# The low part of K on all 128 partitions, and a smaller copy of V that shares a buffer

## The chip, the cores and the metric

The kernel runs on one core of a Trainium2 chip. The metric is device time in microseconds (us), the median of several executions; lower is better.

## The reference, cut to what matters

A trunk of two layers on 1024 tokens of width 1024, float32. Layer 0 is a short gated convolution beside a state-space scan, layer 1 is attention with a forget gate; each is followed by a layer norm, a convolutional feed-forward network and another layer norm. The change touches layer 1 alone:

```
h = x @ w_in                                  # q, k, v of 16 heads of 64, and a forget logit per head
cum = cumsum(log_sigmoid(f_logit + b_f))      # per head, along the tokens
s = (q . k) / 8 + cum[query] - cum[key]       # keys after the query masked
o = softmax(s) @ v                            # per head
mixer = o @ w_out
```

## The kernel before, in words

**Operands.** TensorE multiplies float32r operands. Each float32 operand of a large product is held as the sum of a high and a low part; a projection makes three products (high by high, high by low, low by high).

**Attention.** `attention` takes the 16 heads in 8 pairs. `projections` (L610) computes q, k and v of a pair as [128 channels, 1024 tokens], two heads of 64 channels one above the other, in halves of 512 tokens, each half in one PSUM bank (`place`). `evacuations` (L572) turns such a half into operands:
- q: for each head a tile of 128 partitions, the high part on the head's own 64, the low part on the other 64.
- k: for each head a tile `kh` whose 64 rows of the high part stand on both halves of the partitions (L599, L600), and one tile `kl` for the pair, with each head's low part on the head's own 64 partitions.
- v: a copy `vc` on ScalarE (L586), four transposes on TensorE (L589), and the split into a high and a low part.

`scores(pr, e, i)` (L646) makes the scores of 128 queries (tile i, 0 to 7) of head e of pair pr against the first (i + 1) * 128 keys, in parts of up to 512 columns. A first pass multiplies q's tile of 128 rows by `kh`, which gives q times the high part of K. A second pass multiplies 64 rows, q's high part, by `kl`. A last product of 128 columns adds the causal mask (L660). All go to the one buffer `wide`, which VectorE reads at L663 (bias added, minimum taken); ScalarE takes the exponential, GpSimd divides by the sum.

`weigh` transposes these probabilities in groups of up to four through two small PSUM buffers (`sm`) and splits them into `p`, high on ScalarE and low on VectorE. `values` (L688) multiplies them by v, through the same small buffers; ScalarE copies half of the result to a scratch `ot` (L701), and VectorE adds the other half to it (L702).

**Order.** A loop over the 128 tiles issues the scores of tile n, the transposes of tile n - 2 (`LAG`), and P @ V of tile n - 4 (`VLAG`); steps of four products from the projections, and in the last pair from part of the output projection, are put between them (36 steps a pair, running `LEAD` = 12 steps ahead). The order of the instructions on each engine is then settled by the tile scheduler when the program is built, which may move independent instructions past each other; in the trace, P @ V stands between the scores and the mask of some tiles. Each engine runs its own instructions in order.

**Buffers.** A tag of a pool has a fixed number of slots. Before: `kl` two of 4 KB a partition, `vc` one of 4 KB, `ot` two of 1 KB; `kh` and `q` three of 4 KB each. `places_of` (L745) gives the slots that the last projections and heads leave free to the operands of the output projection's last pairs.

Of the kernel before, what the change touches and what calls it, by code (L numbers as in the profile page):

```python
# [10 lines left out]
F32 = mybir.dt.float32  # L11
F32R = mybir.dt.float32r
# [17 lines left out]
LAG, VLAG = 2, 4    # tiles of 128 tokens by which the transposes and P @ V follow the scores  # L30
XLAG = 2            # tiles by which the transposes into x.T follow the layer norm
LEAD = 12           # steps by which the projections run ahead of the heads
FILL, FILL7 = 36, 72  # steps of products between the heads of a pair, and of the last pair


class Net:
    """The trunk. Every float32 operand of a large product is held as the exact sum of
    two float32r parts, high and low; a product takes the passes hh, hl and lh."""
# [56 lines left out]
    def split(self, high, low, src, engine=None):  # L95
        """high + low == src exactly."""
        self.nc.scalar.copy(high, src)  # L97
        (engine or self.nc.vector).tensor_sub(low, src, high.bitcast(F32))  # L98
# [19 lines left out]
    def project(self, *srcs):  # L118
        """[128 channels, L] = W[:, 128 channels].T @ x.T for each slice of W; several go
        side by side over the rows of x.T."""  # L120
        nc = self.nc
        ws = [src if isinstance(src, (tuple, list)) else self.weight(src) for src in srcs]
        ps = [self.mm_ps() for _ in srcs]
        steps = [(half, k, t, n) for k in range(KD) for t in range(len(srcs)) for n in range(3) for half in range(2)]
        if self.fresh > 0:
            self.fresh -= len(srcs)
            steps.sort(key=lambda s: s[0])
        for half, k, t, n in steps:
            if half:
                while self.after:  # L130
                    self.after.pop(0)()
            h, l = ws[t]
            w, x = ((h, self.xh), (h, self.xl), (l, self.xh))[n]
            hs = slice(half * 512, half * 512 + 512)
            nc.tensor.matmul(ps[t][:, hs], lhsT=w[:, k * P:(k + 1) * P], rhs=x[:, k, hs],  # L135
                             start=(k == 0 and n == 0), stop=(k == KD - 1 and n == 2))
        return ps if len(srcs) > 1 else ps[0]

    def conv(self, out, ps, w, bias=None):
        """Causal depthwise convolution along the free axis; w[:, K] by channel."""  # L140
        nc = self.nc
        K = w.shape[-1]
        if bias is None:
            nc.scalar.activation(out, ps, AF.Copy, scale=w[:, K - 1:K])
        else:
            nc.scalar.activation(out, ps, AF.Identity, scale=w[:, K - 1:K], bias=bias)  # L146
        for s in range(1, K):
            nc.vector.scalar_tensor_tensor(out=out[:, s:], in0=ps[:, :L - s], scalar=w[:, K - 1 - s:K - s],  # L148
                                           in1=out[:, s:], op0=ALU.mult, op1=ALU.add)

    def down(self, ys, ws, evac, late=0):
        """evac(i, psum) for each tile i of 128 tokens of y @ W; what it returns is called after the
        products of the next tile or, after the last tiles, beside the next projection. The last ones
        of ys may come late."""
        nc = self.nc
        n = len(ys)
        blocks = [range(3)] + [[i] for i in range(3, NT)] if late else [[i] for i in range(NT)]
        after = self.after
        for block in blocks:
            ps = {i: self.mm_ps() for i in block}  # L160
            for js in (range(n - late), range(n - late, n)):
                for i in block:
                    for j in js:
                        (yh, yl), (wh, wl) = ys[j], ws[j]
                        for m, (y, w) in enumerate(((yh, wh), (yh, wl), (yl, wh))):
                            for hs in (slice(0, 512), slice(512, D)):
                                nc.tensor.matmul(ps[i][:, hs], lhsT=y[:, i * P:(i + 1) * P], rhs=w[:, hs],  # L167
                                                 start=(j == 0 and m == 0), stop=(j == n - 1 and m == 2))
            while len(after) > XLAG - 1:
                after.pop(0)()  # L170
            after += [then for then in [evac(i, ps[i]) for i in block] if then]

    def log1p_exp_neg_abs(self, x, tmp):
        """log1p(exp(-|x|)) / 2, by 2 atanh(e / (2 + e))."""
        nc, V = self.nc, self.nc.vector
        e, d, z, p = tmp
        nc.scalar.activation(e, x, AF.Abs)
        nc.scalar.activation(e, e, AF.Exp, scale=-1.0)
        V.tensor_scalar_add(d, e, 2.0)
        V.reciprocal(d, d)  # L180
        V.tensor_mul(d, d, e)
        V.tensor_mul(z, d, d)
        V.tensor_scalar_mul(p, z, 1.0 / 17)
        for c in (15, 13, 11, 9, 7, 5, 3):
            V.scalar_tensor_tensor(out=p, in0=p, scalar=1.0 / c, in1=z, op0=ALU.add, op1=ALU.mult)
        V.scalar_tensor_tensor(out=p, in0=p, scalar=1.0, in1=d, op0=ALU.add, op1=ALU.mult)
        return p
# [6 lines left out]
    def thin_weight(self, src, into):  # L194
        """The 16 columns of W as the first of 128, the others zero."""
# [7 lines left out]
    def token_major_16(self, ps, t):  # L203
        """[128, (tile of 128 tokens, 16)] from [16 channels, L]; t: [128, L] of scratch."""
# [14 lines left out]
    def layer_norm(self, r, ps, rsum, lg, lb, spare=None):  # L219
        """In place on r[128 tokens, D], with its sums over D; ps is free for scratch."""  # L220
# [74 lines left out]
    def mixer0(self):  # L295
# [17 lines left out]
        with ExitStack() as s1:  # L313
            cq = s1.enter_context(tc.tile_pool(name="cq", bufs=1))
            xs = [self.rp.tile([P, D], F32, tag=f"r{c}", name=f"xs{c}") for c in range(NT)]
            with ExitStack() as s2:
# [5 lines left out]
                # dt and the decays, [128 steps, chunk, head]  # L322
# [30 lines left out]
                # x, B, C  # L353
# [73 lines left out]
                # gated short convolution, with the scan beside it  # L427
# [14 lines left out]
            # gate  # L442
# [31 lines left out]
            # output projection  # L474
# [45 lines left out]
    def attention(self, r_in):  # L520
# [8 lines left out]
        with tc.tile_pool(name="fox", bufs=1) as fp:  # L529
# [11 lines left out]
            # cumulative log forget gates  # L541
# [30 lines left out]
            def evacuations(pr, kind, n, ps):  # L572
                """Half n of the projection in its bank, as the operands of the heads 2 pr and 2 pr + 1."""
                h = half[n]
                if n == 0:
                    if kind == "v":
                        tiles["vc"] = fp.tile([P, L], F32, tag="vc", name="vc", bufs=1)
                        tiles[pr, "v"] = fp.tile([P, NT, 2, P], F32R, tag="v", name="v", bufs=2)
                    elif kind == "k":
                        tiles[pr, "kl"] = fp.tile([P, L], F32R, tag="kl", name="kl", bufs=2)  # L580
# [3 lines left out]
                if kind == "v":  # L584
                    vc, v = tiles["vc"], tiles[pr, "v"]
                    nc.scalar.copy(vc[:, h], ps)  # L586
                    yield
                    for c in range(4):
                        nc.tensor.transpose(ps[:, c * P:(c + 1) * P], vc[:, (4 * n + c) * P:(4 * n + c + 1) * P], self.ident)  # L589
# [6 lines left out]
                for e, (a, b) in enumerate(sides):  # L596
                    if kind == "k":
                        kh, kl = tiles[pr, "kh"][e], tiles[pr, "kl"]
                        self.split(kh[a, h], kl[a, h], ps[a])  # L599
                        nc.scalar.copy(kh[b, h], ps[a])  # L600
                    else:
# [8 lines left out]
            def projections():  # L610
                """All of q, k and v, in steps of a few products, each half evacuated beside the next."""
# [34 lines left out]
            def scores(pr, e, i):  # L646
                q, kh, kl = [tiles[pr, kind] for kind in ("q", "kh", "kl")]
                n = (i + 1) * P
                ts = slice(i * P, n)
                es = slice(e * 64, e * 64 + 64)  # L650
# [5 lines left out]
                for m, (a, k) in enumerate(((q[e], kh[e]), (q[e][es], kl[es]))):  # L656
                    for bs in parts:
                        nc.tensor.matmul(wide[:, bs], lhsT=a[:, ts], rhs=k[:, bs], start=(m == 0),  # L658
# [29 lines left out]
            def values(pr, e, g):  # L688
# [11 lines left out]
                ot = fp.tile([64, 256], F32, tag="ot", name="ot", bufs=2)  # L700
# [10 lines left out]
            def output_projection():  # L711
                """alpha x + o @ W of the heads 0 to 7 on x_d, in steps of a few products."""
# [33 lines left out]
            def places_of(j):  # L746
                """Slots for the parts of y and W of pair j that the last projections and heads leave free."""
# [4 lines left out]
                elif j == 5:  # L752
                    v = fp.tile([P, 2, L], F32R, tag="v", name="late", bufs=2)
                    t = [own("kl", 2), own("vc", 1), v[:, 0], v[:, 1]]
                elif j == 6:
                    t = [own("q", 3), own("kh", 3)] + weights()
                else:
                    t = [own("p", 4), own("p", 4), own("kl", 2), own("q", 3)]
# [34 lines left out]
            # the rest of the output projection  # L793
# [33 lines left out]
def _inputs(a):  # L827
    """The arrays as the chip reads them: tiles of 128 rows or columns, each contiguous."""
# [57 lines left out]
```

## Time and profile before

| | |
|---|---|
| Median of 3 runs | 2899.41 us (2898.84 to 2900.05) |
| Span of the profiled execution | 2901.4 us; no other time of that execution is given |
| TensorE busy | 2867.8 us (99% of the span) |
| VectorE, ScalarE, GpSimd busy | 1525.6, 918.5, 173.0 us |
| Chain that ended last | PE 91%, DVE 5%, ACT 1%, DMA 1%, issue 1% |
| Products of the attention's projections (L621), busy | 159.1 + 158.0 + 154.4 us |
| Scores' products (L658), share of the chain | 3% |

PE is TensorE's products, PEld its weight loads, DVE VectorE, ACT ScalarE, POOL GpSimd, SP SyncE. Busy times of products overlap: the record of one runs on past the start of the next. PEclk is the clock granted to TensorE, as a share of 2.4 GHz.

### The profile page before, as it was taken

What the parts mean: (1) busy time and instruction counts of PE and PEld (TensorE: products, weight loads), DVE (VectorE), ACT (ScalarE), POOL (GpSimd) and SP (SyncE); (2) the same over time, 40 slices, a digit from 0 to 9 for tenths busy, and PEclk for the clock granted to TensorE, in tenths of its full rate; (3) what the DMA queues carried; (4) which work ended last, traced back from release to release, by engine and by line L of the source; (5) the groups of instructions that cost most, each with busy time, mean ns of one, the idle gap of its engine ahead of it and who ended that gap; (6) DMA issues with size and microseconds to landing.
All of it is one profiled execution on the core that took longest, in us unless ns stands there. A gap on an engine that the chain in (4) does not pass through costs nothing.

```text
span 2901.4 us, 32466 instructions
## 1 busy us (share of the span) xinstructions
PE 2867.8 (99%) x13378; PEld 2328.2 (80%) x13378; DVE 1525.6 (53%) x2085; ACT 918.5 (32%) x1346; POOL 173.0 (6%) x176
## 2 busy tenths in 40 slices
PE   8999999999999999999999999999899999999998
PEld 7888888888788888888887777777687888888887
DVE  4545564444644444554475555555575444444446
ACT  4521111321322222222235555555333222222222
POOL 0000000000000000000002222222100000000000
PEclk9999999999999999999999999999999999999999
DMA  3112221352011111111111111111532111111111
GB/s 136 44 66 81 75 78 66 131 189 87 22 51 56 57 48 51 51 44 44 59 73 53 52 52 44 45 44 51 182 124 73 44 44 44 51 52 57 51 37 73
DMA packets 56771, 194.50 MB, mean 67 GB/s; under 512 B 9392, under 2 KB 9776, under 8 KB 56624
## 3 DMA queue, kind: packets, MB, share of 16 engines
q1 hardware_dynamic: 56624, 192.44, 18.8%
q8 instruction: 105, 1.72, 0.2%
q14 instruction: 42, 0.34, 0.0%
HBM read 167.64 MB, written 24.77 MB: 66 GB/s over the span
## 4 chain that ended last, share of the span: by engine, by line
PE 91%; DVE 5%; ACT 1%; DMA 1%; issue 1%; POOL 0%; SPq 0%; POOLq 0%; ACTq 0%; DVEq 0%
PE mm L135 50%; PE mm L167 20%; PE mm L621 8%; PE mm L658 3%; PE sm L698 3%; PE sm L682 2%; PE mm L660 1%; PE sm L403 1%; PE mm L729 1%; DVE r L230 1%; DVE r L227 1%; DVE s L663 1%; ACT mm L226 1%; PE sm L414 0%; PE sm L409 0%
## 5 line engine op out<-in xcount | busy, mean ns | idle before, releaser
L135 PE MATMUL mm<-xh,wh 128*128 128x512 f32 x2112 | 667.7, 393 | 9.0 <-ACT xh L97 6.9
L135 PE MATMUL mm<-xh,wl 128*128 128x512 f32 x2112 | 663.0, 391 | 0.1
L135 PE MATMUL mm<-xl,wh 128*128 128x512 f32 x2112 | 661.4, 391 | 0.0
L98 DVE TENSOR_TENSOR wl<-wraw,wh 128x1024 fp32r<-128x1024 f32 x217 | 265.4, 1224 | 643.1 <-ACT wh L97 642.6
L97 ACT CAST wh<-wraw 128x1024 fp32r<-128x1024 f32 x217 | 228.0, 1051 | 1123.2 <-PE mm L135 927.3
L135 PEld LDWEIGHTS mm<-xh,wh 128*128 128x128 f32 x2112 | 395.6, 188 | 96.4 <-ACT xh L97 7.8
L135 PEld LDWEIGHTS mm<-xh,wl 128*128 128x128 f32 x2112 | 396.8, 188 | 86.2 <-issue 2.9
L135 PEld LDWEIGHTS mm<-xl,wh 128*128 128x128 f32 x2112 | 397.3, 188 | 84.8 <-issue 1.7
L282 DVE SCALAR_TENSOR_TENSOR r<-r,mm 128x1024 f32<-128x1024 f32 x160 | 195.0, 1219 | 134.1 <-PE mm L167 130.4
L167 PE MATMUL mm<-wh,yh 128*128 128x512 f32 x832 | 260.0, 392 | 0.3
L167 PE MATMUL mm<-wl,yh 128*128 128x512 f32 x832 | 256.8, 390 | 0.0
L167 PE MATMUL mm<-wh,yl 128*128 128x512 f32 x832 | 256.2, 389 | 0.0
L148 DVE SCALAR_TENSOR_TENSOR ug<-mm,ffn_cw,ug 128x1022 f32<-128x1022 f32 (+1 forms) x176 | 224.3, 1277 | 10.8 <-ACT ug L146 9.2
L167 PEld LDWEIGHTS mm<-wh,yh 128*128 128x128 f32 x832 | 153.9, 188 | 36.3 <-issue 5.1
L167 PEld LDWEIGHTS mm<-wh,yl 128*128 128x128 f32 x832 | 156.2, 188 | 32.7
L167 PEld LDWEIGHTS mm<-wl,yh 128*128 128x128 f32 x832 | 156.1, 188 | 32.6
L668 POOL TENSOR_TENSOR s<-s,sum 128x128 f32<-128x128 f32 (+7 forms) x128 | 147.8, 1155 | 459.0 <-DVE sum L667 412.0
L621 PE MATMUL mm<-xh,wh 128*128 128x512 f32 x384 | 159.1, 414 | 0.0
L621 PE MATMUL mm<-xh,wl 128*128 128x512 f32 x384 | 158.0, 412 | 0.0
L621 PE MATMUL mm<-xl,wh 128*128 128x512 f32 x384 | 154.4, 402 | 0.0
L663 DVE CUSTOM_DVE_ANT_0 s<-mm,cb 128x128 f32<-128x128 f32 (+7 forms) x128 | 96.5, 754 | 77.5 <-PE mm L660 61.1
L98 DVE TENSOR_TENSOR p<-sm,p 128x512 fp32r<-128x512 f32 (+1 forms) x192 | 105.5, 554 | 35.8 <-ACT p L97 33.9
(225 smaller groups left out, 2937.3 us busy)
## 6 DMA issues: line engine op xcount, KB each, us to landing
wraw<-in_ffn_w_up SPq DMA_DIRECT2D x88, 512.0 KB, 3.4
wraw<-in_sc_ssm_w_in SPq DMA_DIRECT2D x44, 512.0 KB, 3.5
wraw<-in_ffn_w_down SPq DMA_DIRECT2D x44, 512.0 KB, 3.4
wraw<-in_fox_w_in SPq DMA_DIRECT2D x24, 512.0 KB, 3.4
R<-acs_d SPq DMA_DIRECT2D x16, 512.0 KB, 3.6
wraw<-in_sc_ssm_w_out SPq DMA_DIRECT2D x16, 512.0 KB, 3.8
cb<-cum_d SPq DMA_DIRECT2D x16, 512.0 KB, 3.6
xraw<-in_xT SPq DMA_DIRECT2D x8, 512.0 KB, 9.3
```

The source lines that it names most:

```text
L97: self.nc.scalar.copy(high, src)
L98: (engine or self.nc.vector).tensor_sub(low, src, high.bitcast(F32))
L135: nc.tensor.matmul(ps[t][:, hs], lhsT=w[:, k * P:(k + 1) * P], rhs=x[:, k, hs], start=(k == 0 and n == 0), stop=(k == KD - 1 and n == 2))
L148: nc.vector.scalar_tensor_tensor(out=out[:, s:], in0=ps[:, :L - s], scalar=w[:, K - 1 - s:K - s], in1=out[:, s:], op0=ALU.mult, op1=ALU.add)
L167: nc.tensor.matmul(ps[i][:, hs], lhsT=y[:, i * P:(i + 1) * P], rhs=w[:, hs], start=(j == 0 and m == 0), stop=(j == n - 1 and m == 2))
L282: nc.vector.scalar_tensor_tensor(out=r[i], in0=r[i], scalar=ALPHA if first else 1.0, in1=ps, op0=ALU.mult, op1=ALU.add, **({"accum_out": r ...
L621: nc.tensor.matmul(place, lhsT=a[:, k * P:(k + 1) * P], rhs=x[:, k, half[n]], start=(m == 0), stop=(m == KD * 3 - 1))
L658: nc.tensor.matmul(wide[:, bs], lhsT=a[:, ts], rhs=k[:, bs], start=(m == 0), stop=(m == 1 and bs.stop < n))
L663: V.tensor_tensor_reduce(out=s[:, :n], in0=wide[:, :n], in1=cb[:, :n], op0=ALU.add, op1=ALU.min, scale=1.0, scalar=3e38, accum_out=mn)
L668: nc.gpsimd.tensor_tensor(s[:, :n], s[:, :n], sm.broadcast_to([P, n]), op=ALU.mult)
L682: nc.tensor.transpose(tp[:, c * P:(c + 1) * P], s[:, (b + c) * P:(b + c + 1) * P], self.ident)
L698: nc.tensor.matmul(ops[:, cs], lhsT=v[:, j, e, :], rhs=pt[j // 4 * 2 + m][:, j % 4, cs], start=(j == 0 and m == 0), stop=(j == 2 * g + 1 a ...
```

## The change

- Each head of a pair gets its own low tile of K, and ScalarE copies the 64 rows of the low part to the other half of the partitions as well. The tag `kl` has three slots in place of two.
- The second pass of the scores multiplies all 128 rows of q's tile (high and low part) by this tile, in place of 64 rows.
- `vc` holds one half of 512 tokens (2 KB a partition) in place of 1024, a new tile for each half; the scratch `ot` takes the same single slot.
- The late operands of the output projection's pair 5 take two `kl` slots, in place of one `kl` and the `vc`.
- Comments and docstrings are left out; that changes no instruction.

```
                     elif kind == "k":
-                        tiles[pr, "kl"] = fp.tile([P, L], F32R, tag="kl", name="kl", bufs=2)
+                        tiles[pr, "kl"] = [fp.tile([P, L], F32R, tag="kl", name="kl", bufs=3) for _ in range(2)]
...
                 if kind == "v":
-                    vc, v = tiles["vc"], tiles[pr, "v"]
-                    nc.scalar.copy(vc[:, h], ps)
+                    vc, v = fp.tile([P, 512], F32, tag="vc", name="vc", bufs=1), tiles[pr, "v"]
+                    nc.scalar.copy(vc, ps)
                     yield
                     for c in range(4):
-                        nc.tensor.transpose(ps[:, c * P:(c + 1) * P], vc[:, (4 * n + c) * P:(4 * n + c + 1) * P], self.ident)
+                        nc.tensor.transpose(ps[:, c * P:(c + 1) * P], vc[:, c * P:(c + 1) * P], self.ident)
...
                     if kind == "k":
-                        kh, kl = tiles[pr, "kh"][e], tiles[pr, "kl"]
+                        kh, kl = tiles[pr, "kh"][e], tiles[pr, "kl"][e]
                         self.split(kh[a, h], kl[a, h], ps[a])
                         nc.scalar.copy(kh[b, h], ps[a])
+                        nc.scalar.copy(kl[b, h], kl[a, h].bitcast(F32))
...
             def scores(pr, e, i):
-                q, kh, kl = [tiles[pr, kind] for kind in ("q", "kh", "kl")]
+                q, kh, kl = [tiles[pr, kind][e] for kind in ("q", "kh", "kl")]
...
-                for m, (a, k) in enumerate(((q[e], kh[e]), (q[e][es], kl[es]))):
+                for m, k in enumerate((kh, kl)):
                     for bs in parts:
-                        nc.tensor.matmul(wide[:, bs], lhsT=a[:, ts], rhs=k[:, bs], start=(m == 0),
+                        nc.tensor.matmul(wide[:, bs], lhsT=q[:, ts], rhs=k[:, bs], start=(m == 0),
                                          stop=(m == 1 and bs.stop < n))
...
-                ot = fp.tile([64, 256], F32, tag="ot", name="ot", bufs=2)
+                ot = fp.tile([64, 256], F32, tag="vc", name="ot", bufs=1)
...
-                    t = [own("kl", 2), own("vc", 1), v[:, 0], v[:, 1]]
+                    t = [own("kl", 3), own("kl", 3), v[:, 0], v[:, 1]]
...
-                    t = [own("p", 4), own("p", 4), own("kl", 2), own("q", 3)]
+                    t = [own("p", 4), own("p", 4), own("kl", 3), own("q", 3)]
```

## Rows read from the trace of the kernel before

**Rows 1.** The page: span, and busy time of each engine (share of the span)
```profile
span 2901.4 us, 32466 instructions
...
PE 2867.8 (99%) x13378; PEld 2328.2 (80%) x13378; DVE 1525.6 (53%) x2085; ACT 918.5 (32%) x1346; POOL 173.0 (6%) x176
```

**Rows 2.** Stretches: a steady pair, the last pair; PE, PEld, DVE, ACT, POOL, clock, DMA, GB/s
```profile
1885.00:1954.00 69.00, 68.75 (x372) 53.61 (x372) 40.32 (x94) 39.73 (x84) 18.38 (x16) 1.00 0.13 47
...
2023.00:2107.00 84.00, 76.55 (x363) 58.31 (x363) 47.92 (x92) 34.15 (x64) 16.27 (x13) 0.96 0.52 175
```

**Rows 3.** Waits, 1528 to 2107 us: waiting line, releaser, total us, times, longest
```profile
PEld mm L658 <- issue: 29.6, 109, 0.7
PEld mm L660 <- issue: 22.6, 84, 0.7
```

**Rows 4.** TensorE's timeline, tiles 2 and 3: start us, us, instruction, count merged
```profile
1745.62 0.34 PE L658 MATMUL mm<-kh,q 128*128 128x384 f32 x1
...
1746.26 1.64 PE L698 MATMUL sm<-p,v 128*128 128x256 f32 x12
1747.73 0.27 PE L660 MATMUL mm<-maskr,identr 128*128 128x128 f32 x1
1747.84 0.30 PE L682 MATMUL sm<-ident,s 128*128 128x128 f32 x1
...
1748.91 0.40 PE L658 MATMUL mm<-kh,q 128*128 128x512 f32 x1
1749.24 0.49 PE L658 MATMUL mm<-kl,q 64*128 64x512 f32 x1
1749.66 0.33 PE L660 MATMUL mm<-maskr,identr 128*128 128x128 f32 x1
1749.83 0.40 PE L682 MATMUL sm<-ident,s 128*128 128x128 f32 x2
...
1755.44 0.39 PE L621 MATMUL mm<-xl,wh 128*128 128x512 f32 x1
...
1756.83 0.39 PE L621 MATMUL mm<-xl,wh 128*128 128x512 f32 x1
```

**Rows 5.** The same timeline: tiles 0, 4, 6, 7, first row and row after mask
```profile
1739.42 0.22 PE L658 MATMUL mm<-kh,q 128*128 128x128 f32 x1
...
1739.99 0.45 PE L621 MATMUL mm<-xh,wh 128*128 128x512 f32 x1
...
1753.82 0.45 PE L658 MATMUL mm<-kh,q 128*128 128x512 f32 x2
...
1754.84 0.52 PE L682 MATMUL sm<-ident,s 128*128 128x128 f32 x3
...
1762.37 0.57 PE L658 MATMUL mm<-kh,q 128*128 128x512 f32 x2
...
1763.63 0.45 PE L621 MATMUL mm<-xh,wl 128*128 128x512 f32 x1
...
1767.94 0.61 PE L658 MATMUL mm<-kh,q 128*128 128x512 f32 x2
...
1769.31 0.62 PE L682 MATMUL sm<-ident,s 128*128 128x128 f32 x4
```

**Rows 6.** ScalarE's groups, 1528 to 2107 us: count, busy us, mean ns, idle before
```profile
L600 ACT CAST kh<-mm 64x512 fp32r<-64x512 f32 x32 | 18.6, 582 | 18.9 <-DVE kl L98 18.7
```

**Rows 7.** Waits, 1528 to 2107 us, ScalarE for VectorE in K's evacuation
```profile
ACT kh L600 <- DVE kl L98: 18.7, 25, 1.4
```

**Rows 8.** Timeline of all engines around the start of a head
```profile
1737.68 1.00 PEld L698 LDWEIGHTS sm<-p,v 128*128 128x128 f32 x8 [0.45 <-DVE p L98]
...
1739.33 0.42 DVE L702 TENSOR_TENSOR o<-sm,ot 64x256 f32<-64x256 f32 x1 [0.40 <-ACT ot L701]
...
1739.62 0.59 ACT L586 COPY vc<-mm 128x512 f32<-128x512 f32 x1 [0.33 <-PE mm L621]
...
1742.34 0.60 PE L589 MATMUL mm<-ident,vc 128*128 128x128 f32 x4
```

More of the change, by code (lines that the diff above doesn't have):

```diff
@@ L576, in evacuations @@
                     if kind == "v":
-                        tiles["vc"] = fp.tile([P, L], F32, tag="vc", name="vc", bufs=1)
                         tiles[pr, "v"] = fp.tile([P, NT, 2, P], F32R, tag="v", name="v", bufs=2)
                     elif kind == "k":
-                        tiles[pr, "kl"] = fp.tile([P, L], F32R, tag="kl", name="kl", bufs=2)
+                        tiles[pr, "kl"] = [fp.tile([P, L], F32R, tag="kl", name="kl", bufs=3) for _ in range(2)]
                         tiles[pr, "kh"] = [fp.tile([P, L], F32R, tag="kh", name="kh", bufs=3) for _ in range(2)]
@@ L646, in scores @@
             def scores(pr, e, i):
-                q, kh, kl = [tiles[pr, kind] for kind in ("q", "kh", "kl")]
+                q, kh, kl = [tiles[pr, kind][e] for kind in ("q", "kh", "kl")]
                 n = (i + 1) * P
                 ts = slice(i * P, n)
-                es = slice(e * 64, e * 64 + 64)
                 if i == 0:
```

## The prediction, made before the result was known

> **What bounds the kernel now.** The page comes first. TensorE is busy 2867.8 of 2901.4 us [rows 1], so a change pays only where it shortens TensorE's own row or makes it wait. Busy time is not work, though: a product's record runs on past the start of the next one, so what it costs has to be read from start to start.
>
> The table of stretches comes second, because the change touches only the attention stage. One pair of heads in the steady part is a stretch of 69 us: TensorE 68.75, VectorE 40.32, ScalarE 39.73, clock 1.00 [rows 2]. The two evacuating engines idle some 29 us each; TensorE alone sets the pace. The last pair differs: 84 us, TensorE busy only 76.55 of them, DMA share 0.52, mean clock 0.96 [rows 2]. There TensorE waits for transfers and for the engines that split what they bring.
>
> Third, the waits of that stage. The weight loads of L658 (scores) and L660 (mask) stand idle 29.6 and 22.6 us until "issue": nothing that the profile sees releases them [rows 3]. This is TensorE's own doing, and the timeline of one head shows how. Tile 3 (512 keys): high product at 1748.91, low product (64 rows) at 1749.24, mask at 1749.66, next instruction at 1749.83 [rows 4]. So 0.33 + 0.42 + 0.17 = 0.92 us for three products. Products of the same width on 128 rows follow each other at (1756.83 - 1755.44) / 6 = 0.23 us, and the twelve of P @ V in tile 2, most of 256 columns, at (1747.73 - 1746.26) / 12 = 0.12 us [rows 4]. Tile 2 holds a control: its mask comes after 128-row products, and what follows starts 0.11 us later instead of 0.17 [rows 4]. Hence the extra time sits where the 64-row product is entered, run and left.
>
> **The change part by part.**
>
> *Both passes on 128 rows.* The number of products stays: per tile the high ones, as many low ones, one mask. Prices on 128 rows: 0.23 (512 columns), 0.12 (256), 0.11 (128, the control); for 384 I take 0.17, between its neighbours (an estimate). Tile by tile, from the start of the first high product to the start of what follows the mask:
> - tile 0 (128): 1739.99 - 1739.42 = 0.57 [rows 5]; after, 3 x 0.11 = 0.33; saves 0.24
> - tile 2 (384): 1746.26 - 1745.62 = 0.64 without the mask [rows 4]; after, 0.34; saves 0.30 (its mask is cheap already)
> - tile 3 (512): 0.92; after, 0.23 + 0.23 + 0.11 = 0.57; saves 0.35
> - tile 4 (512 + 128): 1754.84 - 1753.82 = 1.02 [rows 5]; after, 2 x 0.34 + 0.11 = 0.79; saves 0.23
> - tile 6 (512 + 384): 1763.63 - 1762.37 = 1.26 [rows 5]; after, 2 x 0.40 + 0.11 = 0.91; saves 0.35
> - tile 7 (512 + 512): 1769.31 - 1767.94 = 1.37 [rows 5]; after, 4 x 0.23 + 0.11 = 1.03; saves 0.34
> - tiles 1 and 5 follow transposes, after which a product is recorded a little early, so their readings blur; I give them 0.34, as tiles 6 and 7.
>
> One head saves 0.24 + 0.34 + 0.30 + 0.35 + 0.23 + 0.34 + 0.35 + 0.34 = 2.49 us, 16 heads 39.8 us. That the low pass now also multiplies the low part of q costs nothing beyond this: products and columns stay the same in number.
>
> A rule speaks against this term. The Trainium skill, "TensorE: Matmul & The Clock Gate", section "Why this matters for your kernels", says that a single product with 32 rows takes the same time as one with 128, the gain of fewer rows lying in running several at once. By it the second pass would cost the same afterwards and the sum would be nothing. The spacings above disagree, 0.42 against 0.23 us; the rule is the second rival.
>
> *The copy of the low part.* Each half of a K projection now has, for each of its two heads, one more ScalarE copy, 64x512 from SBUF: 8 pairs x 2 halves x 2 heads = 32. The nearest row is the copy of the high part onto the other partitions, 0.582 us [rows 6], so 18.6 us of ScalarE, 2.3 per pair against 29 idle. Its input is VectorE's subtraction, but ScalarE already waits for that one before the existing copy (25 times, 18.7 us in all [rows 7]), so the new copy finds it done; queued behind it are the exponentials and the copies of the transposed probabilities, which TensorE waits for through the two small PSUM buffers. By the code the projections run 12 steps of four products ahead of the heads, so the copy itself is not awaited. Bounds: 0, if it all falls into idle time; 32 x 0.582 = 18.6 us, if every copy shifts TensorE in full. I take 0, by the idle share. (The Trainium skill, "ScalarE: Activation LUTs", section "What ACT_TABLE_LOAD costs", gives 186 ns + 0.833 ns per element without pointer operands: 0.61 us by that page, an estimate, and 19.6 us in place of 18.6.)
>
> *K-low tiles, three slots for two per pair.* The second head's low tile takes the slot that the first head of the pair before leaves. The high tiles of K have the same three slots and are written just ahead of it, so that wait, where there is one, is already over. Cost 0; it would be paid twice only if the high tile did not wait first.
>
> *V's copy and the output's scratch in one slot.* The copy of V must now wait until the last addition out of the scratch is read. In the head shown that addition runs from 1739.33 to 1739.75, the copy starts at 1739.62: it comes 0.13 us later. The transposes that read it start at 1742.34 [rows 8], 2.1 us after its end, so nothing reaches TensorE. The scratch in turn waits for those transposes, and no products of P @ V come between copy and transposes here. Cost 0; upper bound 16 x 0.13 = 2.1 us. The late slots of pair 5 move from V's copy to a K-low slot free since the first head of the last pair ended: 0.
>
> *What is late next.* Once per head TensorE waits for VectorE's low part of P, 0.45 us before the eight products at 1737.68 [rows 8]; it comes soon after tile 7's scores. If the wait grows by all that tile 7 saves, 16 x 0.34 = 5.4 us go back. But the work it waits for is itself released by those scores, so it mostly moves along; between 0 and 5.4 I take 2.0. In the last pair, where transfers set the pace, I take half of its two heads' saving as lost: 2.5 us (bounds 0 and 5.0).
>
> Sum: 39.8 - 0 - 2.0 - 2.5 = 35.3 us. The profiled execution spans 2901.4 us, and no other time of it is given; 2901.4 - 35.3 = 2866.1. The median of the runs is 2899.41, 2.0 below that span; so I expect **2864.1 us**.
>
> **The rivals.**
> 1. *The saving turns into waits for the evacuating engines.* For it: the wait of 0.45 us is already there, and ScalarE gets new work in the steps before a head changes. Against it: both engines idle over 40%. All copies in full and the whole growth of the wait: 18.6 + 5.4 + 2.5 = 26.5, leaving 13.3 us: 2886.1.
> 2. *The change doesn't do what it says: 64 rows are not the cause, and the same spacing stays.* For it: the page's rule. Against it: the control in tile 2. Gain 0: 2899.4.
> 3. *Slower, through the clock.* In the last pair, TensorE's clock stood at half for a while after waits: 0.04 of 84 us, so 6.7 us at 1.2 GHz and 3.4 us lost [rows 2]. If the shorter scores lengthen the wait at each head's end so that the clock falls there too, it costs 16 x 3.4 = 54.4 us: 2864.1 + 54.4 = 2918.5. It outweighs the gain from the eleventh such stretch on. Against it: at 0.45 us per head the clock now stays at 1.00.
> 4. *More than forecast.* No loss in waits, and the slow stretch of the last pair gone: 39.8 + 3.4 = 43.2: 2856.2.
>
> **How the numbers follow.** Forecast 0.75, rival 1 0.10, rival 2 0.03, rival 3 0.04, rival 4 0.08. The range takes in rival 4 and half the way to rival 1's waits: 2855 to 2880. A measurement of this kernel tells about 0.2% (5.8 us) from no change. The forecast and rivals 1 and 4 are faster by more: 0.93. Within: 0.03. Slower: 0.04.
>
> **What would show it.** Right: the scores' products all 128*128; tile 3's three products in about 0.57 us and tile 7's in 1.03; the loads' idle at "issue" nearly gone; 32 new copies of about 0.6 us; a pair of 64 us where 69 stood. Wrong: low products still 0.33 us or more apart at 512 columns (rival 2); waits at the small PSUM buffers grown by microseconds per head, with ScalarE ahead of them (rival 1); a clock below 1.00 in the middle pairs (rival 3). The forecast fails as a whole if a pair still takes over 67 us.

## The result, and the profile after

The changed kernel takes 2866.23 us (median of 4 runs, 2865.14 to 2867.84) against 2899.26 us before: 33.0 us less, ratio 0.9884, 95% interval 0.987 to 0.9898. Forecast were 2864.1 us and a range of 2855 to 2880. Run again beside other kernels it gave 2865.69 against 2900.59 us, 34.9 us less, with the same ratio (interval 0.9867 to 0.99). The profiled execution spans 2863.2 us and took 2865.14.

The page of the changed kernel, with its span and busy times. TensorE is 46 us less busy [rows 1], ScalarE 16 us more:

```profile
span 2863.2 us, 32454 instructions
...
PE 2821.5 (99%) x13378; PEld 2328.4 (81%) x13378; DVE 1525.9 (53%) x2085; ACT 934.9 (33%) x1378; POOL 172.8 (6%) x176
```

The stretches that answer to [rows 2], a steady pair and the last one, columns as there. VectorE does what it did and ScalarE 1.8 us more, in 64 us instead of 69:

```profile
1848.00:1912.00 64.00, 62.78 (x370) 53.39 (x369) 40.28 (x93) 41.53 (x88) 18.35 (x16) 1.00 0.14 50
...
1986.00:2069.00 83.00, 72.95 (x376) 59.70 (x375) 49.17 (x94) 34.36 (x65) 16.63 (x14) 0.98 0.54 177
```

A pair's time is read more sharply from the mask products: 97 of them lie from tile 0 of a pair to tile 0 of the sixth pair after it. The rows give their number, the least, median and longest time of one in ns, and the first and last start, for the kernel before and the changed kernel:

```profile
L660 PE MATMUL mm<-maskr,identr x97: 273/327/332, 1602.6 to 2014.3; 128*128 128x128 f32 x97
```
```profile
L659 PE MATMUL mm<-maskr,identr x97: 221/224/279, 1595.6 to 1979.6; 128*128 128x128 f32 x97
```

That is 411.7 / 6 = 68.6 us a pair before, 384.0 / 6 = 64.0 after: 4.6 us a pair. (The first mask of the stage also comes 2.3 us earlier, at 1527.3 instead of 1529.6, though nothing ahead of it was changed. In the runs below that leave that part alone it comes at 1526.9 to 1528.0, so the profiled execution of before had lost 2 us by then. The spans differ by 38.2 us and the medians by 33 to 35; these 2 us are a part of that, and the profiled execution of the changed kernel, 1.1 us under its median, is another.)

The waits of the stage, as in [rows 3]. No row of the scores' or the mask's loads until "issue" is left, and TensorE waits for VectorE's low part of P at two kinds of places, P @ V (L697, 1.9 us before) and the transposes (L681, no such row of its products before):

```profile
PE sm L697 <- DVE p L98: 6.8, 15, 1.3
...
PE sm L681 <- DVE p L98: 3.0, 6, 0.5
```

TensorE's timeline of a head, as in [rows 4, 5]: tiles 0, 2, 3, 4, 6 and 7, three places where it waits, the last of them in tile 1 of the next head:

```profile
1720.68 0.48 PE L621 MATMUL mm<-xh,wl 128*128 128x512 f32 x1
1721.66 1.16 PE L697 MATMUL sm<-p,v 128*128 128x256 f32 x8 [0.51 <-DVE p L98]
...
1723.40 0.22 PE L657 MATMUL mm<-kh,q 128*128 128x128 f32 x1
...
1723.68 0.45 PE L621 MATMUL mm<-xh,wh 128*128 128x512 f32 x1
...
1728.02 0.40 PE L621 MATMUL mm<-xl,wh 128*128 128x512 f32 x1
1728.50 0.66 PE L681 MATMUL sm<-ident,s 128*128 128x128 f32 x4
...
1729.22 0.33 PE L657 MATMUL mm<-kh,q 128*128 128x384 f32 x1
...
1729.57 1.53 PE L697 MATMUL sm<-p,v 128*128 128x256 f32 x12
1730.93 0.28 PE L659 MATMUL mm<-maskr,identr 128*128 128x128 f32 x1
...
1732.12 0.40 PE L657 MATMUL mm<-kh,q 128*128 128x512 f32 x1
1732.36 0.39 PE L657 MATMUL mm<-kl,q 128*128 128x512 f32 x1
1732.59 0.22 PE L659 MATMUL mm<-maskr,identr 128*128 128x128 f32 x1
1732.64 0.39 PE L681 MATMUL sm<-ident,s 128*128 128x128 f32 x2
...
1736.62 0.45 PE L657 MATMUL mm<-kh,q 128*128 128x512 f32 x2
...
1737.37 0.51 PE L681 MATMUL sm<-ident,s 128*128 128x128 f32 x3
...
1744.49 0.56 PE L657 MATMUL mm<-kh,q 128*128 128x512 f32 x2
...
1745.30 0.22 PE L659 MATMUL mm<-maskr,identr 128*128 128x128 f32 x1
1745.36 0.45 PE L621 MATMUL mm<-xh,wl 128*128 128x512 f32 x1
...
1749.69 0.62 PE L657 MATMUL mm<-kh,q 128*128 128x512 f32 x2
...
1750.67 0.60 PE L681 MATMUL sm<-ident,s 128*128 128x128 f32 x4
...
1758.64 0.22 PE L659 MATMUL mm<-maskr,identr 128*128 128x128 f32 x1
1759.37 0.63 PE L681 MATMUL sm<-ident,s 128*128 128x128 f32 x4 [0.50 <-DVE p L98]
```

Tile 3 takes 0.24 + 0.23 + 0.05 = 0.52 us, where it took 0.92. Tiles 0, 2, 4, 6 and 7 take 0.28, 0.35 (without the mask), 0.75, 0.87 and 0.98: they save 0.29, 0.29, 0.27, 0.39 and 0.39. With 0.39 for tiles 1 and 5 as well, that is 2.81 us a head. Tile 2 saves 0.11 more behind these products: the twelve of P @ V take 1.36 us (1729.57 to 1730.93), where they took 1.47 [rows 4]. So a head saves 2.92 us and a pair 5.8. Of these 4.6 arrive; 1.2 us a pair goes into waits.

Three places show these waits. The kernel before has at two of them:

```profile
1737.07 0.48 PE L621 MATMUL mm<-xh,wl 128*128 128x512 f32 x1
...
1744.72 0.39 PE L621 MATMUL mm<-xl,wh 128*128 128x512 f32 x1
...
1744.95 0.60 PE L682 MATMUL sm<-ident,s 128*128 128x128 f32 x4
```

P @ V starts 0.98 us after the product ahead of it (1720.68 to 1721.66), where it was 0.61 (1737.07 to 1737.68 [rows 8]) and 0.23 is the normal spacing. In tile 1 of a pair's first head, transposes start 0.48 us after a product (1728.02 to 1728.50), not 0.23. The transposes after the mask of tile 1 of the second head start 0.73 us after it (1758.64 to 1759.37), not 0.05 to 0.11. That is some 0.37 + 0.25 + 0.64 = 1.3 us, by these rows.

The new copy on ScalarE, and its queue near the end of a pair:

```profile
L600 ACT CAST kl<-kl 64x512 fp32r<-64x512 f32 x32 | 19.8, 618 | 0.6
```
```profile
1654.27 0.61 PE L681 MATMUL sm<-ident,s 128*128 128x128 f32 x4
...
1654.94 0.62 ACT L600 CAST kl<-kl 64x512 fp32r<-64x512 f32 x1
...
1655.57 0.58 ACT L97 CAST kh<-mm 64x512 fp32r<-64x512 f32 x1
...
1656.18 0.59 ACT L97 CAST p<-sm 128x512 fp32r<-128x512 f32 x1
...
1656.91 0.69 DVE L98 TENSOR_TENSOR p<-sm,p 128x512 fp32r<-128x512 f32 x1
```

Its price, 0.618 us, agrees with the 0.61 us estimated in the prediction from the Trainium skill, "ScalarE: Activation LUTs", section "What ACT_TABLE_LOAD costs". The transposes of 1654.27 are copied only at 1656.18, behind the new copy and one of K's high part; the subtraction that frees their buffer ends at 1657.60, and P @ V waits for that buffer.

### The profile page after: what moved, and what is told of

It reads as the page before. It is cut to its first block, busy times and chain, and to the rows that moved or that the text cites. A ratio compares the mean times of both kernels' runs of the same rounds, so it can differ in the third digit from the quotient of the medians.

```text
span 2863.2 us, 32454 instructions
## 1 busy us (share of the span) xinstructions
PE 2821.5 (99%) x13378; PEld 2328.4 (81%) x13378; DVE 1525.9 (53%) x2085; ACT 934.9 (33%) x1378; POOL 172.8 (6%) x176
## 4 chain that ended last, share of the span: by engine, by line
PE 88%; DVE 6%; ACT 3%; DMA 1%; issue 1%; POOL 0%; SPq 0%; POOLq 0%; ACTq 0%; DVEq 0%
PE mm L135 51%; PE mm L167 21%; PE mm L621 7%; PE sm L697 2%; PE mm L657 2%; PE sm L681 1%; PE sm L403 1%; PE mm L728 1%; DVE p L98 1%; DVE r L230 1%; DVE r L227 1%; ACT mm L226 1%; DVE wl L98 0%; PE sm L414 0%; PE sm L409 0%
## 5 line engine op out<-in xcount | busy, mean ns | idle before, releaser
L665 ACT ACTIVATE s<-s,mn 128x128 f32<-128x128 f32 (+7 forms) x128 | 99.4, 776 | 49.9 <-DVE mn L662 48.2
```

What stands on the lines that cost most here:

```text
L665: nc.scalar.activation(s[:, :n], s[:, :n], AF.Exp, scale=-1.0, bias=mn, accum_out=sm)
```

## The experiments

**Which part brings the gain.** The changed kernel with the second pass back on 64 rows, the copies, tiles and slots kept:

```
-                for m, k in enumerate((kh, kl)):
+                es = slice(e * 64, e * 64 + 64)
+                for m, (a, k) in enumerate(((q, kh), (q[es], kl[es]))):
...
-                        nc.tensor.matmul(wide[:, bs], lhsT=q[:, ts], rhs=k[:, bs], ...
+                        nc.tensor.matmul(wide[:, bs], lhsT=a[:, ts], rhs=k[:, bs], ...
```

> The changed kernel with its second pass of the scores taken back to 64 rows (the head's own half of its low tile): the new ScalarE copies, the low tile per head and the shared slot stay. Theory (the whole gain is TensorE's, from the 128 rows): 2899 to 2903 us, as before, plus at most 3 us for the copies. Rival (part of the gain comes from the new tiles or slots): below 2890 us.

Measured: 2901.36 us beside 2901.0 for before, ratio 1.0 (0.9991 to 1.0009). First and last mask of six pairs:

```profile
L660 PE MATMUL mm<-maskr,identr x97: 273/328/330, 1600.5 to 2012.4; 128*128 128x128 f32 x97
```

411.9 / 6 = 68.6 us a pair. The whole gain is the 128 rows; on 64 rows the copies cost nothing.

**The shared slot alone.** The kernel before with the halved copy of V and the scratch in its slot:

```
+                    vc, v = fp.tile([P, 512], F32, tag="vc", name="vc", bufs=1), tiles[pr, "v"]
...
+                ot = fp.tile([64, 256], F32, tag="vc", name="ot", bufs=1)
...
+                    t = [own("kl", 2), own("late", 1), v[:, 0], v[:, 1]]
```

> The kernel before with only the smaller copy of V and the scratch of P @ V in one slot (the late operand that used V's slot gets one of its own). Theory (the copy of V comes up to 0.13 us later and its transposes 2 us after): 2899 us, no difference. Rival (the one slot makes ScalarE wait and TensorE with it): 2902 us or more.

Measured: 2901.56 beside 2901.0, ratio 1.0003 (0.9994 to 1.0012). It costs nothing that can be measured. (The reverse, the changed kernel with a scratch of its own, was not tried.)

**Where the 64-row product pays.** First, the high pass on 64 rows too:

```
-                for m, (a, k) in enumerate(((q[e], kh[e]), (q[e][es], kl[es]))):
+                for m, (a, k) in enumerate(((q[e][es], kh[e][es]), (q[e][es], kl[es]))):
```

> The kernel before with the first pass of the scores on 64 rows too (high part of q times high part of K); the product of q's low part with K's high part is left out. Theory (every 64-row product pays for its own weight load, and entering from 128 rows and leaving cost about 0.1 us each): 0.1 us more in tiles 0 to 3, 0.2 us more in tiles 4 to 7, 1.2 us a head, 19 us: 2918 us. Rival (only the change between 64 and 128 rows costs, and there are as many as before): 2899 us. The rule that rows don't matter: 2899 us too.

Measured: 2903.67 beside 2901.0, ratio 1.0009 (1.0 to 1.0019): 2.7 us, not 19. The theory fell. Its timeline, tiles 3 and 7:

```profile
1747.82 0.40 PE L621 MATMUL mm<-xh,wh 128*128 128x512 f32 x1
1748.14 0.49 PE L658 MATMUL mm<-kh,q 64*128 64x512 f32 x1
1748.48 0.39 PE L658 MATMUL mm<-kl,q 64*128 64x512 f32 x1
1748.81 0.33 PE L660 MATMUL mm<-maskr,identr 128*128 128x128 f32 x1
1748.97 0.41 PE L682 MATMUL sm<-ident,s 128*128 128x128 f32 x2
...
1767.23 0.72 PE L658 MATMUL mm<-kh,q 64*128 64x512 f32 x2
1767.80 0.63 PE L658 MATMUL mm<-kl,q 64*128 64x512 f32 x2
1768.35 0.33 PE L660 MATMUL mm<-maskr,identr 128*128 128x128 f32 x1
```

From the last 128-row product to the end of the mask: 0.32 + 0.34 + 0.33 + 0.16 = 1.15 us, with two 64-row products. Before, with one, the same sum is 0.24 for the product ahead (from 1748.67, between the rows shown) and 0.92 [rows 4]: 1.16. The extra time has moved from the high product to the product ahead of it, and a second 64-row product adds none. Tile 7 says the same: its four 64-row products take 1.12 us to the mask, the two of tile 3 take 0.67, so two more cost 0.45, the normal 0.23 each. The price seems to hang on going from 128 rows to 64 and back, once a tile. If so, going twice must cost twice. The kernel before with its two loops exchanged makes tiles 4 to 7 go there and back twice, with the same products:

```
-                for m, (a, k) in enumerate(((q[e], kh[e]), (q[e][es], kl[es]))):
-                    for bs in parts:
+                for bs in parts:
+                    for m, (a, k) in enumerate(((q[e], kh[e]), (q[e][es], kl[es]))):
```

> The kernel before with the two loops of the scores exchanged: part by part, each part's high and low product together. The products are the same; tiles 4 to 7, which have two parts, go from 128 to 64 rows and back twice in place of once. Theory now (the price hangs on the change between 64 and 128 rows, some 0.3 us for there and back, however many 64-row products stand between): 64 tiles x 0.3 = 19 us more, 2919 us, about 1.2 us more a head. Rival (each 64-row product pays for itself): 2900 us, as before.

Measured: 2923.8 beside 2900.63, ratio 1.008 (1.0063 to 1.0097): 23.2 us for 64 more round trips, 0.36 each. The theory held, with a price above its 0.3. Six pairs, and tile 4:

```profile
L660 PE MATMUL mm<-maskr,identr x97: 276/328/329, 1604.2 to 2035.0; 128*128 128x128 f32 x97
```
```profile
1761.78 0.39 PE L658 MATMUL mm<-kh,q 128*128 128x512 f32 x1
1762.09 0.49 PE L658 MATMUL mm<-kl,q 64*128 64x512 f32 x1
1762.52 0.33 PE L658 MATMUL mm<-kh,q 128*128 128x128 f32 x1
1762.77 0.32 PE L658 MATMUL mm<-kl,q 64*128 64x128 f32 x1
1763.03 0.33 PE L660 MATMUL mm<-maskr,identr 128*128 128x128 f32 x1
1763.19 0.52 PE L682 MATMUL sm<-ident,s 128*128 128x128 f32 x3
```

Tile 4 takes 1.41 us, where it took 1.02 [rows 5]: 0.39 for the second trip. A pair takes 430.8 / 6 = 71.8 us, 3.2 more, or 0.40 for each of its eight extra trips. That is the 0.40 us which tile 3 saves in the changed kernel. (The exchanged order was not run on 128 rows. Taking turns between operands is not by itself dear there: the projections' products change one operand or both each time and follow each other at 0.23 us.)

**What the waits come from.** The changed kernel without the copies; the second pass reads the high tile again:

```
-                        nc.scalar.copy(kl[b, h], kl[a, h].bitcast(F32))
...
-                for m, k in enumerate((kh, kl)):
+                for m, k in enumerate((kh, kh)):
```

> The changed kernel without the 32 copies; the second pass reads the high tile of K once more, so the low part of K is left out of the scores. TensorE's work is that of the changed kernel. Theory (the copies delay the first transposed probabilities at the end of each pair's second head by about 0.4 us): 2863 us, 3 us under the changed kernel. Rival 1 (the copies fall into idle time, as predicted): 2866 us. Rival 2 (they cost all of their time): 2866 - 20 = 2846 us.

Measured: 2863.41 us, ratio to before 0.9872 (0.9859 to 0.9886). Six pairs, and the place ahead of P @ V:

```profile
L658 PE MATMUL mm<-maskr,identr x97: 220/226/278, 1595.6 to 1977.9; 128*128 128x128 f32 x97
```
```profile
1720.54 0.48 PE L620 MATMUL mm<-xh,wl 128*128 128x512 f32 x1
1721.17 1.14 PE L696 MATMUL sm<-p,v 128*128 128x256 f32 x8 [0.16 <-DVE p L98]
```

382.3 / 6 = 63.7 us a pair; P @ V now starts 0.63 us after the product ahead instead of 0.98. The copies cost 0.3 us a pair at this place, some 2.3 us in all; the waits in tile 1 of both heads are still there. The same copies on GpSimd:

```
-                        nc.scalar.copy(kl[b, h], kl[a, h].bitcast(F32))
+                        nc.gpsimd.tensor_copy(kl[b, h], kl[a, h].bitcast(F32))
```

> The changed kernel with the 32 copies of the low part on GpSimd in place of ScalarE. Theory (on ScalarE they hold up the transposed probabilities by 0.3 us a pair; on GpSimd they run beside): a pair in 63.7 us, 2864 us. Rival (GpSimd takes 1 us and more for a copy and holds up its own division of the probabilities, which TensorE's transposes wait for): 2866 us or slower.

> The changed kernel once more, as the measure for the runs beside it: 2866 us, a pair of heads in 64.0 us.

Measured on one chip: the changed kernel 2865.69 us (2864.02 to 2868.87), this one 2862.8 (2861.06 to 2863.63). Six pairs, and the copy:

```profile
L659 PE MATMUL mm<-maskr,identr x97: 221/226/278, 1595.0 to 1977.0; 128*128 128x128 f32 x97
```
```profile
L600 POOL CAST kl<-kl 64x512 fp32r<-64x512 f32 x32 | 19.5, 608 | 61.3 <-DVE kl L98 60.4
```

382.0 / 6 = 63.7 us a pair: the theory held, and GpSimd copies as fast as ScalarE. For the other 0.9 us a pair, the low parts of the projections' weights went from VectorE to GpSimd, with ScalarE's copies of K kept and then moved too:

```
             def projections():
...
+                self.low_engine = nc.gpsimd
                 ready, pending = self.weight(win[work[0][2]]), iter(())
...
+                self.low_engine = V
                 for _ in pending:
                     yield
```

> The changed kernel with the subtraction that makes the low part of the projections' weights (128x1024, 1.23 us each, three a pair) on GpSimd in place of VectorE. Theory (what the shorter scores gave back, 1 us a pair, are waits for low parts of P queued on VectorE behind other subtractions, the one of 0.6 us in tile 1 of the second head behind a weight's): a pair in 63.4 us, 2862 us. Rival 1 (the waits come from the chain of transposes, copy and subtraction itself, whatever else VectorE has to do): 2866 us. Rival 2 (GpSimd's division comes too late): 2868 us or slower.

> Both: weights' low parts and copies of K's low part on GpSimd. Theory: the two savings add, 2860 us. Rival (GpSimd becomes late): 2866 us or slower.

Measured: 2866.66 and 2864.6 us, a pair in 63.9 and 63.6. The 0.73 us after the mask of the second head's tile 1 shrink to 0.16, but the transposes behind it start 0.52 us after a product, 0.29 in the changed kernel, and the wait in the first head's tile 1 stays at 0.48. The order of TensorE's instructions is another one too: in that head P @ V stands between the high and the low product of tile 2. The stage starts some 3 us later; a weight's subtraction takes 2.40 us on GpSimd and 1.22 on VectorE, but that this is the reason was not shown. No gain. So VectorE's other subtractions seem to be a part of that one wait and not all of it; with the order changed as well, the runs do not separate the two. What else holds TensorE there was not taken apart.

**The version to keep.** Both copies of K onto the other half on GpSimd, the high part's from SBUF:

```
-                        nc.scalar.copy(kh[b, h], ps[a])
-                        nc.scalar.copy(kl[b, h], kl[a, h].bitcast(F32))
+                        nc.gpsimd.tensor_copy(kh[b, h], kh[a, h].bitcast(F32))
+                        nc.gpsimd.tensor_copy(kl[b, h], kl[a, h].bitcast(F32))
```

> The changed kernel with both copies of K onto the other half of the partitions on GpSimd, the high part's too, now read from SBUF and not from PSUM. Theory (ScalarE's queue at the end of a pair's second head costs TensorE 0.3 us a pair, and the copy of the low part was all of it): a pair in 63.7 us, 2862 to 2863 us, as with the low part's copy alone on GpSimd. Rival (the copy of the high part holds up as much again): a pair in 63.4 us, 2860 us. Rival 2 (GpSimd becomes late): 2866 us.

Measured: 2862.04 us (2861.67 to 2863.85) beside 2900.63, ratio 0.9866 (0.9852 to 0.9881), a pair in 63.6 us, nearer the theory's 63.7 than the rival's 63.4. It is the fastest median of all, but its interval overlaps that of the low copy alone on GpSimd (0.987, 0.9855 to 0.9885).

## Why the prediction was right, point by point

*The 128 rows.* The cause was right and the term too small: 46.7 us (16 x 2.92), not 39.8. The price put too high was the mask's: I gave it 0.11 us, from a mask between short products, but after one of 384 or 512 columns it takes 0.05 to 0.06 (1732.59 to 1732.64, 1745.30 to 1745.36). And in tile 2 the P @ V behind the 64-row product held 0.11 us of the price, which the prediction read as P @ V's own 0.12 us a product.

*Where the time sat.* The prediction put it on the 64-row product "entered, run and left". Entering and leaving is right, running is not: among 64-row products the spacing at 512 columns is normal (two more in 0.45 us). Tile 3 shows where the 0.40 us were: 0.09 on the 128-row product ahead, 0.19 on the 64-row product, 0.12 on the mask behind it. The "0.42 against 0.23 us" held against the Trainium skill's rule compared a product that pays for going to 64 rows with one that doesn't. The rule, that a product with 32 rows takes the time of one with 128, agrees with what the runs show for 64 rows after all: with the high product on 64 rows in place of 128, tile 3 takes 1.15 us against 1.16. Rival 2, built on it, fell all the same, since what the change removes is not the time of a product. The Trainium skill, "TensorEngine Tiling (Array Packing)", section "Key Properties", says that a change of the tiling mode drains TensorE. The 0.36 to 0.40 us for there and back would fit that; that TensorE drains there, no run shows by itself.

*The copies: 0.* They cost some 2.3 us, 0.3 us in each pair (the run with them on GpSimd was 2.9 us faster), at the one place where ScalarE's queue leads to a buffer that TensorE waits for. ScalarE's idle share was the wrong measure: 22 us of a 64 us pair are idle, and not those.

*What is late next: 2.0.* About 6.5 us (0.9 us a pair, 0.25 + 0.64 by the rows above), and not where I put it. Without the copies the wait ahead of P @ V is as before (0.63 us after the product ahead, 0.61 before); the new ones stand in tile 1 of both heads. The profile puts them down to VectorE's low part of P; that shorter scores no longer cover it is argued, not shown.

*The last pair: half lost.* From the first mask of the last pair to the last of the stage, 91.96 us before and 88.62 after: 3.3 of 5.8 us arrive. The clock has a share in it: 83 x 0.02 = 1.7 us lost at 1.2 GHz, where it was 3.4, so half of these 3.3 us may be the clock's. This term is not well known: in the profile of the changed kernel run again the same stretch took 87.35 us.

*The slots: 0.* Right.

The gain came out 6.9 us larger than forecast and the copies and waits 6.8 us dearer: 46.7 - 2.3 - 6.5 - 2.5 = 35.4 us, beside 35.3 forecast and 33.0 and 34.9 measured. That the two misses cancel is luck; the waits of 6.5 us are what the pair times leave over, so the sum is bound to come near the measured time. Rival 1 had its mechanism right, and some two fifths of its 26.5 us came; rival 3 did not come, the clock of a steady pair stays at 1.00.

## What to carry to other kernels

A product on 64 rows between products on 128 cost 0.3 to 0.4 us here for going there and back, in a tile of 128 columns as in one of 1024; fill the rows up, or put all that is on 64 rows together. The price is seen start to start and in weight loads that wait for "issue", not in TensorE's busy share, which read 99% throughout. And a copy added to a half idle engine costs what stands behind it at the place where its queue leads to a wait: put it where no such wait stands behind it, here on GpSimd.

## What the runs showed of the hardware that had not been expected

A second 64-row product in a row adds no price of its own, and the extra 0.1 us of entering is booked on the 128-row product ahead (0.32 in place of 0.24 us). GpSimd copies 64x512 from SBUF to SBUF in 0.608 us, ScalarE in 0.618; but its subtraction of 128x1024 takes 2.40 us, VectorE's 1.22.
